# Running sums of a depthwise convolution kept in a PSUM bank instead of SBUF

## The chip, the core and the metric

The kernel runs on one core of one Trainium2 chip. It is a single launch, and the metric is the time on the device in microseconds. The instructions go to five engines that run beside each other and wait for each other through semaphores: TensorE (PE in the rows, PEld for its weight loads), VectorE (DVE), ScalarE (ACT), GpSimd (POOL) and SyncE (SP), which issues transfers.

## The reference, cut to what matters

The program computes two layers of a hybrid block (convolution, retention and window attention side by side, 256 positions, 1024 channels), and behind them a second block with a recurrence, a Fourier mix and a mixture of experts. The change touches one operation of the first two layers, the depthwise convolution of 31 taps:

```python
def conv_module(u_glu, gate, dw, db, ln_g, ln_b):
    a, b = jnp.split(u_glu, 2, axis=-1)
    v = a * jax.nn.sigmoid(b)
    y = lax.conv_general_dilated(
        v, dw[:, None, :].astype(v.dtype), window_strides=(1,),
        padding=[(CONV_KERNEL // 2, CONV_KERNEL // 2)],
        dimension_numbers=('NWC', 'WIO', 'NWC'),
        feature_group_count=CONV_WIDTH) + db.astype(v.dtype)
...
    mu = jnp.mean(yf, axis=-1, keepdims=True)
    var = jnp.mean(jnp.square(yf - mu), axis=-1, keepdims=True)
    yf = (yf - mu) * lax.rsqrt(var + EPS) * ln_g.astype(jnp.float32) + ln_b.astype(jnp.float32)
    y = jax.nn.silu(yf).astype(v.dtype)
    return y * jax.nn.silu(gate)
```

## The kernel before

Channels lie on the 128 partitions and positions along the free dimension, so the 1024 channels are 8 column blocks `k` of 128 × 256. `vpad` holds v of all 8 with 15 zeros at either side, `dw` the taps as per-partition scalars. `conv_taps` takes a pair of column blocks (four pairs `q` in a layer) and adds up 31 shifted products on VectorE: tap 0 is a `tensor_scalar` (product plus bias), taps 1 to 30 are `scalar_tensor_tensor`, out = vpad shifted × scalar + running sum. The running sum `acc[k]` is an SBUF tile; its buffers are called C1_0 to C1_7, and C in the trace. The two column blocks of a pair take turns, so a tap needs the result of the instruction two places ahead of it.

The program is one long list in the order in which a planner (`Sched`) emits it. The main generator (`layer`) emits TensorE's work, weight block by weight block. Beside it run tasks (`spawn`), each a generator that yields between pieces: with priority 0 they bring results out of PSUM, with 1 they are attention and retention chains, and the convolution's tasks have priority 2, the lowest. `pump` steps tasks whose condition holds and whose planned time has come, `force` steps one where the main list waits. The planner holds a cost for each instruction and a finishing time for each engine; what an engine then executes is strictly in the emitted order. Costs depend on where operands lie, and the low halves of the split weights (`wlo` = `wraw` − `whi`) go to VectorE or GpSimd as its times say.

Of the eight PSUM banks four (`pbulk`, tiles pb) take the large products and four (`pside`, tiles ps) serve attention, retention and statistics. `conv_taps` uses none before. Its results are awaited twice: `conv_fin` starts with eight products of `acc` by `ones` on TensorE (a mean over channels), and in the merge the attention output (products of A by `whi` and `wlo`) waits for `pairs + taps`, since its tile takes the place of `vpad`. The gate products (H by `whi` and `wlo`) stand ahead of it. The retention branch (`hd0`, `hd1`) normalises its rows on VectorE with groups of a BN_STATS, a BN_AGGR, a dozen instructions one column wide (`rs_ub`, `rs_yb`) and one that applies it.

Each record of an engine's work goes through one helper, line 192, so the rows are told apart by their tiles.

Of the kernel before, what the change touches and what calls it, by code (L numbers as in the profile page):

```python
# [328 lines left out]
class Kern:  # L329
# [370 lines left out]
        self.tbs.put(sg)  # L700
        self.pbulk.put(pa, pb)

    def conv_taps(self, l, q, glu):
        V, par = self.dve, self.par[l]
        vpad, acc = self.vpad, self.acc
        yield lambda: glu.done
        dwc = lambda j, k: self.dw[l][(j * 8 + k) // 124][:, (j * 8 + k) % 124:(j * 8 + k) % 124 + 1]
        for j in range(31):
            for k in (2 * q, 2 * q + 1):
                if j == 0:  # L710
                    V.tensor_scalar(
                        out=acc[k], in0=vpad[:, k, 0:256], scalar1=dwc(0, k), scalar2=par[:, 32 + k:33 + k],
                        op0=ALU.mult, op1=ALU.add)
                else:
                    V.scalar_tensor_tensor(
                        out=acc[k], in0=vpad[:, k, j:j + 256], scalar=dwc(j, k), in1=acc[k],
                        op0=ALU.mult, op1=ALU.add)
            if j % 2 == 0:
                yield

    def h_tiles(self):
# [334 lines left out]
    def layer(self, l):  # L1056
        s, A, par = self.s, self.A, self.par[l]
# [27 lines left out]
        for c in range(2):  # L1085
            def done(i, pb):
                agt.append(self.evac(self.silu_task(ag[c * 4 + i * 2:c * 4 + i * 2 + 2], pb)))
            yield from self.form_b(h, 8, done)
# [12 lines left out]
        taps, cgt = [], []  # L1101
        for q in range(4):
            got = {}
            def done(i, pb):
                got[i] = pb
                if i == 1:
                    taps.append(s.spawn(self.conv_taps(l, q, self.evac(self.glu_task(q, got[0], got[1]))), 2))
            yield from self.form_b(h, 8, done)
        cg = self.parts("C2")
        for q in range(2):  # L1110
            def done(i, pb):
                cgt.append(self.evac(self.silu_task(cg[4 * q + 2 * i:4 * q + 2 * i + 2], pb)))
            yield from self.form_b(h, 8, done)
# [1952 lines left out]
```

## Time and profile before

| | us |
|---|---|
| median of 3 runs | 2966.68 (2962.86 to 2969.67) |
| the profiled execution's own time | 2963.53 |
| its span | 2961.8 |

| engine | busy us | share of the span | instructions |
|---|---|---|---|
| PE | 2531.1 | 85% | 16380 |
| DVE | 1737.0 | 59% | 3380 |
| POOL | 789.1 | 27% | 544 |
| ACT | 757.3 | 26% | 1307 |

The shares are means over stages with different limits. The two layers take the first 1600 us or so, the experts most of the rest. A stretch is read by which engine is hardly ever idle in it. In the trace's orders of time a row joins equal instructions that follow each other: its first number is the start, its second the time from the first one's start to the last one's end, and x the count. A last bracket names idle time of the engine ahead of it and what ended it.

### The profile page before, as it was taken

Reading aid. Unit: us, or ns where it says so; the run is one execution under the profiler, and the core shown is the slowest. Engines: PE = TensorE matmul, PEld = TensorE weight load, DVE = VectorE, ACT = ScalarE, POOL = GpSimd, SP = SyncE. Lnnn points to the kernel's source line nnn. Section 1 sums busy time; section 2 is a strip of 40 time slices with the busy share of each in tenths; the row PEclk is TensorE's granted clock in tenths of the full one; section 3 lists DMA queues with packets and bytes.
Section 4 is the critical chain, followed back from the end, with each engine's and each line's share of the span. In section 5 each row is a group of like instructions: output and inputs, shape, how many; then the busy total and the mean of one; then the engine's idle time right before and its main releaser. Section 6 shows DMA issues by size and latency. Waiting matters only on the chain. (4 is left out here: it accounts for less than half of the span.)

```text
span 2961.8 us, 43624 instructions
## 1 busy us (share of the span) xinstructions
PE 2531.1 (85%) x16380; PEld 1649.1 (56%) x16380; DVE 1737.0 (59%) x3380; ACT 757.3 (26%) x1307; POOL 789.1 (27%) x544
## 2 busy tenths in 40 slices
PE   6887777679998876788989986699999999999784
PEld 3767656568978765578978564443433323333111
DVE  3769999977458899986466747522332323323213
ACT  2432332244444432334433211110100100001000
POOL 3325444545235454544322214200000000000000
PEclk9888888899999988899988987699999999999987
DMA  7354333334654333335562352489999999999996
GB/s 253 89 206 149 108 93 93 100 106 150 202 170 128 99 107 100 100 114 159 182 237 94 103 145 98 139 323 362 408 409 409 408 406 407 404 405 406 404 407 252
DMA packets 267314, 661.43 MB, mean 223 GB/s; under 512 B 48098, under 2 KB 66030, under 8 KB 265944
## 3 DMA queue, kind: packets, MB, share of 16 engines
q1 hardware_dynamic: 255616, 633.46, 60.0%
q0 software_dynamic: 6240, 22.05, 2.0%
q10 hardware_dynamic: 5240, 3.06, 0.4%
q8 instruction: 131, 2.15, 0.3%
q14 instruction: 87, 0.71, 0.1%
HBM read 640.63 MB, written 17.86 MB: 222 GB/s over the span
## 5 line engine op out<-in xcount | busy, mean ns | idle before, releaser
L192 POOL TENSOR_TENSOR wlo<-wraw,whi 128x1024 fp32r<-128x1024 f32 (+1 forms) x211 | 520.3, 2482 | 653.9 <-ACT whi L192 586.6
L192 PE MATMUL pb<-H,whi 128*128 128x256 f32 x2784 | 551.3, 300 | 31.1 <-ACT whi L192 10.3
L192 PEld LDWEIGHTS pb<-H,whi 128*128 128x128 f32 x2784 | 466.1, 205 | 44.3 <-issue 23.4
L192 ACT CAST whi<-wraw 128x1024 fp32r<-128x1024 f32 (+1 forms) x352 | 359.9, 1041 | 457.0 <-PE pb L192 279.3
L192 PE MATMUL pb<-H,wlo 128*128 128x256 f32 x1392 | 412.2, 296 | 25.3 <-POOL wlo L192 18.7
L192 DVE SCALAR_TENSOR_TENSOR C<-vpad,dw,C 128x256 f32<-128x256 f32 x480 | 350.3, 797 | 0.0
L192 DVE TENSOR_TENSOR wlo<-wraw,whi 128x1024 fp32r<-128x1024 f32 (+1 forms) x141 | 193.1, 1376 | 201.4 <-ACT whi L192 191.1
L192 PEld LDWEIGHTS pb<-H,wlo 128*128 128x128 f32 x1392 | 284.7, 204 | 28.3 <-POOL wlo L192 21.3
L192 POOL TENSOR_TENSOR mf<-mf,mx 128x512 f32<-128x512 f32 x2 | 3.2, 1640 | 1026.7 <-DVE mf L192 1026.7
L192 PE MATMUL pb<-wraw,mx 128*32 128x256 f32 (+1 forms) x1680 | 254.3, 493 | 25.8 <-DMA wraw<-in_w 25.2
L192 PE MATMUL pb<-whi,H 128*128 128x512 f32 x704 | 245.7, 421 | 0.0
L192 PE MATMUL pb<-wraw,maT 128*64 128x512 f32 (+1 forms) x920 | 201.8, 612 | 8.2 <-DMA wraw<-in_w 7.6
L192 PEld LDWEIGHTS pb<-wraw,mx 128*32 128x32 f32 (+1 forms) x1680 | 75.2, 123 | 162.0 <-issue 81.1
L192 ACT ACTIVATE ms<-mg 128x256 f32<-128x256 f32 (+1 forms) x78 | 29.1, 373 | 526.3 <-DVE mg L192 509.8
L192 PEld LDWEIGHTS pb<-whi,H 128*128 128x128 f32 x704 | 141.1, 200 | 35.1 <-issue 3.0
L192 DVE TENSOR_SCALAR mg<-pb 128x256 f32<-128x256 f32 (+1 forms) x59 | 21.8, 369 | 224.8 <-PE pb L192 224.8
L192 PE MATMUL pb<-wlo,H 128*128 128x512 f32 x352 | 145.0, 412 | 7.8 <-POOL wlo L192 7.0
L192 DVE SCALAR_TENSOR_TENSOR my<-pb,msg,my 128x512 fp32r<-128x512 f32 x29 | 21.8, 751 | 170.1 <-ACT my L192 169.6
L192 PEld LDWEIGHTS pb<-wraw,maT 128*64 128x64 f32 (+1 forms) x920 | 47.7, 127 | 122.4 <-issue 63.9
L192 PE MATMUL ps<-cst_base,t 128*128 128x128 f32 x208 | 43.6, 338 | 78.3 <-DVE t L192 46.3
L192 DVE TENSOR_TENSOR mf<-ps,mf 128x512 f32<-128x512 f32 x117 | 76.3, 684 | 54.1 <-PE ps L192 48.7
L192 PE MATMUL ps<-wraw,mx 128*32 128x256 f32 (+1 forms) x568 | 91.9, 506 | 5.8 <-DMA wraw<-in_w 5.6
(652 smaller groups left out, 4302.2 us busy)
## 6 DMA issues: line engine op xcount, KB each, us to landing
wraw<-in_w SPq DMA_DIRECT2D x580, 512.0 KB, 10.1
wraw<-in_w_in SPq DMA_DIRECT2D x228, 512.0 KB, 4.0
whi<-in_w SPq DMA_DIRECT2D x95, 512.0 KB, 10.1
wlo<-in_w SPq DMA_DIRECT2D x93, 512.0 KB
wraw<-in_w_ada SPq DMA_DIRECT2D x48, 512.0 KB, 5.3
wraw<-in_w_in SPq DMA_DIRECT2D x68, 256.0 KB, 3.9
wraw<-in_w_ret_out SPq DMA_DIRECT2D x32, 512.0 KB, 4.0
wraw<-in_w_out SPq DMA_DIRECT2D x24, 512.0 KB, 5.9
```

Of the source, the lines that this page charges most:

```text
L192: r = f(*a, **k)
```

## The change

`conv_taps` takes one bank of `pside`. The running sums of its two column blocks are the two halves of that bank, from tap 0 to tap 29; tap 30 reads them there and writes `acc[k]` in SBUF. The bank is given back behind the last tap. A task starts only when the tasks of the earlier pairs are done (`before`) and a bank of `pside` is free, so that at most one bank is held. The arithmetic is the same, in the same order.

```diff
-    def conv_taps(self, l, q, glu):
+    def conv_taps(self, l, q, glu, before):
+
         V, par = self.dve, self.par[l]
         vpad, acc = self.vpad, self.acc
-        yield lambda: glu.done
+        yield lambda: glu.done and all(k.done for k in before) and len(self.pside.free) > 0
+        ps = self.pside.get()
+        z = {2 * q: ps[:, 0:256], 2 * q + 1: ps[:, 256:512]}
...
                     V.tensor_scalar(
-                        out=acc[k], in0=vpad[:, k, 0:256], scalar1=dwc(0, k), scalar2=par[:, 32 + k:33 + k],
+                        out=z[k], in0=vpad[:, k, 0:256], scalar1=dwc(0, k), scalar2=par[:, 32 + k:33 + k],
...
                     V.scalar_tensor_tensor(
-                        out=acc[k], in0=vpad[:, k, j:j + 256], scalar=dwc(j, k), in1=acc[k],
+                        out=acc[k] if j == 30 else z[k], in0=vpad[:, k, j:j + 256], scalar=dwc(j, k), in1=z[k],
...
             if j % 2 == 0:
+                if j == 30:
+                    self.pside.put(ps)
                 yield
...
-                    taps.append(s.spawn(self.conv_taps(l, q, self.evac(self.glu_task(q, got[0], got[1]))), 2))
+                    taps.append(s.spawn(self.conv_taps(l, q, self.evac(self.glu_task(q, got[0], got[1])), list(taps)), 2))
```

The order changes in the two layers only. VectorE, near the start of the taps in the first layer, with the waits that an instruction has; DVE_49 is VectorE's own semaphore. R are attention's rotated inputs, C the running sums. Before:

```order
L192 SCALAR_TENSOR_TENSOR C_0_1982<-vpad,dw_603,C_0_1982 128x256
L192 SCALAR_TENSOR_TENSOR C_1_1983<-vpad,dw_603,C_1_1983 128x256
L192 SCALAR_TENSOR_TENSOR C_0_1982<-vpad,dw_603,C_0_1982 128x256 [waits DVE_49]
L192 SCALAR_TENSOR_TENSOR C_1_1983<-vpad,dw_603,C_1_1983 128x256 [waits DVE_49]
L192 TENSOR_TENSOR R_0_1924<-R_0_1922,R_1_1923 128x192
```

The same place now:

```order
L192 SCALAR_TENSOR_TENSOR ps_2232<-vpad,dw_603,ps_2232 128x256
L192 SCALAR_TENSOR_TENSOR ps_2232<-vpad,dw_603,ps_2232 128x256 [waits DVE_49] x3
L192 COPY A_0_1647<-ps_2433 128x256 [waits PE_49]
L192 COPY A_1_1648<-ps_2433 128x256
L192 TENSOR_TENSOR R_0_1924<-R_0_1922,R_1_1923 128x192
```

Every tap but the first of a group waits for the tap just ahead of it, also where that one wrote the other half of the bank; before, the third and fourth waited for the first and second.

VectorE at the end of the first layer's taps, before (t are retention's rows, ps products of retention):

```order
L192 SCALAR_TENSOR_TENSOR t_5_5012<-ps_5014,bmv,R_0_4521 128x512
L192 SCALAR_TENSOR_TENSOR C_6_1988<-vpad,dw_605,C_6_1988 128x256
L192 SCALAR_TENSOR_TENSOR C_7_1989<-vpad,dw_605,C_7_1989 128x256
L192 SCALAR_TENSOR_TENSOR C_6_1988<-vpad,dw_605,C_6_1988 128x256
L192 SCALAR_TENSOR_TENSOR C_7_1989<-vpad,dw_605,C_7_1989 128x256
L192 BN_STATS bst<-ps_5139 128x6
```

Now (left out between the rows with "...", two normalisation groups):

```order
L192 SCALAR_TENSOR_TENSOR t_6_4928<-ps_5023,bmv,R_0_4503 128x512
L192 SCALAR_TENSOR_TENSOR ps_4942<-vpad,dw_603,ps_4942 128x256 x8
L192 TENSOR_TENSOR R_0_5146<-ps_5147,R_0_5145 128x512
L192 SCALAR_TENSOR_TENSOR ps_4942<-vpad,dw_603,ps_4942 128x256 x4
L192 TENSOR_TENSOR R_0_5146<-ps_5168,R_0_5145 128x512
L192 SCALAR_TENSOR_TENSOR ps_4942<-vpad,dw_603,ps_4942 128x256 x4
...
L192 SCALAR_TENSOR_TENSOR ps_4942<-vpad,dw_603,ps_4942 128x256 x8
L192 SCALAR_TENSOR_TENSOR t_4_5179<-ps_5185,t_4_5179 128x512
L192 SCALAR_TENSOR_TENSOR ps_4942<-vpad,dw_605,ps_4942 128x256 x12
...
L192 SCALAR_TENSOR_TENSOR ps_4942<-vpad,dw_605,ps_4942 128x256 x12
...
L192 SCALAR_TENSOR_TENSOR ps_4942<-vpad,dw_605,ps_4942 128x256 x6
L192 SCALAR_TENSOR_TENSOR C_6_1988<-vpad,dw_605,ps_4942 128x256
```

With the last one, for C_7, 56 taps of the fourth pair now stand behind the group that ends in t_6; before, the taps of the four pairs were interleaved, and four were left behind the group that ends in t_5.

TensorE at the same place, before (gate products, then `ones`, then more gate products; the attention output follows 24 rows later):

```order
L192 MATMUL pb_5023<-H_817,wlo 128x256
L192 MATMUL ps_5139<-R_0_4519,t_3_4931 128x512 x2
L192 MATMUL ps_5144<-C_0_1982,ones 128x256
...
L192 MATMUL ps_5144<-C_7_1989,ones 128x256
L192 MATMUL pb_5022<-H_817,whi 128x256
```

Now:

```order
L192 MATMUL pb_4992<-H_817,wlo 128x256
L192 MATMUL ps_5147<-cst_base,t_5_4927 128x128
...
L192 MATMUL ps_5185<-R_4159 128x256 x4
L192 MATMUL ps_5205<-R_1_4502,t_4_5179 128x512 x2
L192 MATMUL ps_5241<-R_1_4502,t_4_5179 128x512 x2
...
L192 MATMUL ps_5292<-C_0_1982,ones 128x256
...
L192 MATMUL ps_5292<-C_7_1989,ones 128x256
...
L192 MATMUL pb_5307<-A_0_3425,whi 128x256
```

The gate products all stand ahead of the `ones` now, and between them come only retention's last products; the attention output stands right behind.

## Rows read from the trace of the kernel before

**Rows 1.** Busy time by stretch; columns are named in the first line.

```profile
core 0: us, PE busy (x) PEld busy (x) DVE busy (x) ACT busy (x) POOL busy (x), PEclk, DMA share, GB/s
268.00:635.00 367.00, 267.60 (x1431) 219.57 (x1430) 345.13 (x623) 116.57 (x197) 168.72 (x80) 0.85 0.35 99
635.00:925.00 290.00, 268.69 (x1922) 251.49 (x1921) 184.07 (x278) 128.40 (x179) 126.24 (x70) 0.98 0.53 166
925.00:1290.00 365.00, 284.69 (x1620) 239.05 (x1619) 338.86 (x585) 131.03 (x213) 189.28 (x87) 0.88 0.36 104
```

**Rows 2.** Groups of VectorE instructions: busy us, mean ns, idle time before.

```profile
L192 DVE SCALAR_TENSOR_TENSOR C<-vpad,dw,C 128x256 f32<-128x256 f32 x480 | 350.3, 797 | 0.0
L192 DVE TENSOR_SCALAR C<-vpad,dw,par 128x256 f32<-128x256 f32 x16 | 11.3, 746 | 0.0
```

**Rows 3.** Instructions of tile C: shortest/median/longest ns, first and last start.

```profile
L192 DVE SCALAR_TENSOR_TENSOR C<-vpad,dw,C x480: 465/475/2633, 279.9 to 1287.8; 128x256 f32<-128x256 f32 x160
L192 DVE TENSOR_SCALAR C<-vpad,dw,par x16: 394/404/2483, 268.4 to 1055.5; 128x256 f32<-128x256 f32 x16
L192 DVE TENSOR_TENSOR C<-vpad,C x16: 418/422/427, 782.9 to 1468.7; 128x256 fp32r<-128x256 f32 x16
```

**Rows 4.** VectorE in order of time, runs of taps in the first layer.

```profile
557.90 13.21 DVE L192 SCALAR_TENSOR_TENSOR C<-vpad,dw,C 128x256 f32<-128x256 f32 x12
...
571.63 6.41 DVE L192 SCALAR_TENSOR_TENSOR C<-vpad,dw,C 128x256 f32<-128x256 f32 x16
...
581.75 16.57 DVE L192 SCALAR_TENSOR_TENSOR C<-vpad,dw,C 128x256 f32<-128x256 f32 x20
```

**Rows 5.** GpSimd in order of time, the same stretch.

```profile
559.67 9.97 POOL L192 TENSOR_TENSOR wlo<-wraw,whi 128x1024 fp32r<-128x1024 f32 x4 [4.67 <-ACT whi L192]
583.61 10.07 POOL L192 TENSOR_TENSOR wlo<-wraw,whi 128x1024 fp32r<-128x1024 f32 x4 [13.97 <-ACT whi L192]
```

**Rows 6.** Instructions that read PSUM tiles (ps, pb), columns as in rows 3.

```profile
L192 DVE SCALAR_TENSOR_TENSOR LK<-ps,par,LK x8: 473/480/486, 106.3 to 1561.7; 128x256 f32<-128x256 f32 x8
...
L192 DVE TENSOR_SCALAR tmp<-pb,gb x16: 536/542/545, 53.5 to 1508.3; 128x256 f32<-128x256 f32 x16
L192 DVE SCALAR_TENSOR_TENSOR H<-pb,par,H x16: 474/483/484, 98.7 to 849.4; 128x256 fp32r<-128x256 f32 x16
...
L192 DVE TENSOR_TENSOR C<-pb,tb x16: 401/410/425, 331.6 to 1032.7; 128x256 f32<-128x256 f32 x16
```

**Rows 7.** VectorE in order of time, in the experts.

```profile
2408.13 0.43 DVE L192 SCALAR_TENSOR_TENSOR mg<-ml,mg 128x256 f32<-128x256 f32 x1 [0.21 <-ACT ms L192]
2408.59 0.42 DVE L192 TENSOR_TENSOR ma<-mg,ms 128x256 f32<-128x256 f32 x1
2408.93 0.42 DVE L192 TENSOR_SCALAR mg<-pb 128x256 f32<-128x256 f32 x1
```

**Rows 8.** Instructions that write wlo, columns as in rows 3.

```profile
L192 POOL TENSOR_TENSOR wlo<-wraw,whi x211: 1253/2422/6308, 45.9 to 1581.5; 128x1024 fp32r<-128x1024 f32 x104, 128x512 fp32r<-128x512 f32 x2
L192 DVE TENSOR_TENSOR wlo<-wraw,whi x141: 692/1226/3427, 50.7 to 1853.7; 128x1024 fp32r<-128x1024 f32 x140, 128x512 fp32r<-128x512 f32 x1
```

**Rows 9.** VectorE in order of time, end of the first layer's taps.

```profile
629.59 0.68 DVE L192 BATCH_NORM_STATS2 bst<-ps 128x6 f32<-128x512 f32 x1
...
633.38 1.66 DVE L192 SCALAR_TENSOR_TENSOR C<-vpad,dw,C 128x256 f32<-128x256 f32 x4
```

**Rows 10.** TensorE in order of time: gates, ones and A; A in the second layer.

```profile
625.97 1.16 PE L192 MATMUL pb<-H,whi 128*128 128x256 f32 x2
...
637.07 3.62 PE L192 MATMUL ps<-C,ones 128*128 128x256 f32 x16
...
643.37 0.40 PE L192 MATMUL pb<-A,whi 128*128 128x256 f32 x2
...
1280.80 0.68 PE L192 MATMUL pb<-A,whi 128*128 128x256 f32 x1
```

**Rows 11.** TensorE's groups from 643 to 693 us, columns as in rows 2.

```profile
L192 PE MATMUL ps<-R,t 128*128 128x512 f32 x8 | 3.8, 593 | 0.0
L192 PE MATMUL ps<-cst_base,t 128*128 128x128 f32 x12 | 2.0, 277 | 2.8 <-ACT t L192 2.8
```

## Prediction

> **What bounds the kernel now.** I read the stretches first [rows 1]. From 268 to 635 us (first layer) and from 925 to 1290 us (second), VectorE is busy 345 of 367 us and 339 of 365 us, TensorE only 268 and 285 us: VectorE sets the pace there. In the 290 us behind the first of them it is the other way round: TensorE 269 us, VectorE 184. The changed work, the 31 taps of the depthwise convolution over 8 column blocks, lies entirely in the two stretches: 480 SCALAR_TENSOR_TENSOR and 16 TENSOR_SCALAR [rows 2], 240 and 8 in each layer.
>
> Then I looked at one tap. Its mean is 797 ns, its median 475 and its longest 2633 [rows 2, 3], for always the same shape. The order of time shows why: 16 taps in a row took 6.41 us while GpSimd was idle, 12 took 13.21 us while it ran four `wlo` subtractions of about 2.5 us, and 20 took 16.57 us under four more [rows 4, 5]. A tap that meets a running GpSimd operation waits for its end, some 2 us. The operations of VectorE with one input in PSUM show no such wait, though they run in the same stretches: their longest and shortest times differ by 10 to 24 ns [rows 6]. They include one of the tap's own form, with a per-partition scalar (473 to 486 ns).
>
> **The change part by part**, as time of VectorE, both layers together, against the profiled execution (2963.5 us, span 2961.8; the median of the runs, 2966.7, lies 3.2 us above it).
>
> 1. *The sums are in PSUM, so a tap has one SBUF input and no longer waits for GpSimd.* 480 × (797 − 475) ns = 154.6 us and 16 × (746 − 404) ns = 5.5 us [rows 2, 3]: **−160 us**. The tap itself keeps 475 ns: forms with a PSUM source of this width take 410 to 483 ns [rows 6], those without 422 to 475 [rows 3]. That VectorE writes PSUM is not in this trace; I bound the tap from below by 410 ns and from above by the slowest 256-wide row with a PSUM source, 542 ns [rows 6], which is −31 or +32 us, and take 475, the row that is the same operation. [...]
>
> 2. *Two blocks share one bank, and every tap now waits for the one just ahead of it.* The order shows the wait on nearly every row; before, a tap waited for the one two places ahead. The price is in the start-to-start times: without a wait on its neighbour the next instruction starts before the first has ended (taps: (6.41 − 0.47)/15 = 0.396 us for a tap of 0.475 [rows 3, 4]; the pair 2408.59 and 2408.93 us: 0.34 for 0.42), with it 0.03 to 0.04 us after its end (2408.13 and 2408.59: 0.46 for 0.43) [rows 7]. So a tap takes 0.475 + 0.035 = 0.51 instead of 0.396 us: 480 × 0.114 = **+55 us**. The first of each group has no such wait, which makes 40 the lower end.
>
> 3. *GpSimd still runs.* An operation of 2.42 us [rows 8] that no longer holds up a tap can hold up the next VectorE instruction with two SBUF inputs. Where taps stand in runs of 8 or 12 it ends inside the run; a group of 4 takes 2.0 us and doesn't cover it. I give back a quarter of the 160, **+40 us**; none and half (80) are the ends.
>
> 4. *What the new order puts into the stretch.* The blocks run one after the other, so the last tap of a layer now stands behind three more normalisation groups of the retention branch (3.8 us each, from 629.59 to the next tap at 633.38 [rows 9]) and some 4 us of its other steps: 15 us a layer, +31. The planner also turns 15 `wlo` subtractions in the two stretches over to VectorE: 15 × (1.226 − 0.083) = +17 us [rows 8], and 12 fewer stand on GpSimd there. Four of them held up a run of taps by 13.21 − 12 × 0.40 = 8.4 us, 2.1 each [rows 4, 5]; I take 1.5 for any of them, −18. Together **+30 us**.
>
> 5. *Idle time of VectorE.* Now 22 and 26 us [rows 1]. Its work falls by 160 − 55 − 40 − 30 = 35 us, which brings it near TensorE's in the middle of the stretch; there VectorE will wait for TensorE at times. I take 30 us a layer: **+12**; from −10 to +40.
>
> 6. *The end of the stretch.* Here something new is late. The sums over `acc` (`ones`) need the last tap, and TensorE works in order, so the attention output (`A`) waits behind them. Before, TensorE went from the first gate product at 625.97 through the `ones` at 637.07 to the first `A` product at 643.37, without a pause [rows 10]. Now 56 taps of the last block, two normalisation groups and 4 us of scaling follow the last gate product's neighbours on VectorE: 56 × 0.51 + 7.6 + 4 = 40 us, with TensorE nearly idle: `A` starts some 38 us later behind the gates than before. VectorE's time for this is in the terms above already; it only lies in one place. What comes on top: in the first layer 8.3 us stood between the end of the last tap (633.38 + 1.66 [rows 9]) and `A`, for gate products, and in the new order only the `ones` and four transposes, some 4.6 (−4). In the second layer `A` started at 1280.8, ahead of the last tap's start at 1287.8 [rows 3, 10], and will start 4.6 us behind its end (+14): **+10 us**.
>
> 7. *Behind it.* The retention steps that moved ahead are gone from the stretch that TensorE bounds: in the first 50 us of it they held TensorE 2.0 + 3.8 us and stood in most of its pauses [rows 11], and a few microseconds return: −6 us a layer, **−12 us**.
>
> Sum: −160 + 55 + 40 + 30 + 12 + 10 − 12 = **−25 us**; 2963.5 − 25 = 2938.5, and on the scale of the medians **2942 us**. From about 1600 us on both programs have the same order; nothing changes there.
>
> **The rivals.**
>
> *The turn at the bank costs more than the speed brings (slower).* The mechanism is term 6: early blocks that are done faster don't help if TensorE can't use the time before the last block. The sum of −25 is made of +76 at the ends of the two layers (38 each), −12 behind them and so −89 ahead of them. If TensorE, busy 73 and 78% of the stretches [rows 1], or the attention chains, which have one bank fewer, let only 60% of the 89 through, 36 us are missing: 2978. It decides as soon as more than 25 of the 89 are lost. For it: that share of TensorE. Against it: the granted clock is only 0.85 and 0.88 there [rows 1], so TensorE's work has some room to shrink.
>
> *The waits move to other instructions (no change).* Term 3 at 40% instead of 25% is +24 us: 2966. For it: other VectorE work is about half of the stretch. Against it: many of its instructions read PSUM and can't be held up [rows 6].
>
> *The semaphore between neighbours costs nothing (faster).* Then term 2 is gone: 2942 − 55 = 2887. The rows speak against it [rows 7]. [...]
>
> *A tap into PSUM is slow (slower).* At 542 ns, the upper bound of term 1, the time is 2942 + 32 = 2974.
>
> *The change doesn't do what it says.* If a tap with one SBUF input still waits for GpSimd, since its scalar also lies in SBUF, the 160 stays and the quarter of term 3 falls away: 2942 + 160 − 40 = 3062. The forms with such a scalar and no spread [rows 6] speak against it.
>
> **How the numbers follow.** Chances: forecast, 2915 to 2957, 0.52; turn at the bank 0.20; waits move 0.14; no cost of the semaphore 0.05; slow tap 0.05; no effect 0.04. A change of 0.2% (6 us) is about what a measurement of this kernel can tell from none. Faster: 0.48 of the forecast and the 0.05, 0.53. Same: 0.04 of the forecast, 0.05 of the bank's turn, 0.11 of the moved waits, 0.02 of the slow tap, 0.22. Slower: the rest of these, 0.15 + 0.03 + 0.03, and 0.04, 0.25. The range for 8 in 10 reaches from the forecast with less given back by GpSimd's operations (2942 − 37 = 2905) to the bank's turn with some of the slower tap (2982). The forecast's own range, 2915 to 2957, stands beside it.
>
> **What would show it.** In the profile after: the median and the mean of a tap near each other (475 to 485 ns; a longest of over 1 us refutes term 1); runs of taps at 0.51 us from start to start (0.40 refutes term 2); other VectorE instructions with two SBUF inputs waiting longer in sum than now, by some 40 us; a pause of TensorE of 30 to 45 us ahead of the `ones` products of both layers, with VectorE busy; the first `A` product some 10 to 20 us earlier than 643 us. If `A` comes later than 643 us, term 3 or 5 was too small, and the bank's turn has decided.

## The result and the profile after

The changed kernel takes 2910.57 us (median of 4 runs, 2907.73 to 2912.84); the kernel before, run beside it, 2964.77. The ratio is 0.9824 (0.9809 to 0.9838): 48 to 57 us faster, where the prediction had 25.

The stretches of the profiled execution (2911.1 us; columns as in [rows 1]): first to last tap of the first layer, from there to the first tap of the second, its taps, and from its last tap to 1554.7 us, where the last product of H by `whi` of the program starts, some 100 us into the second block (1606.3 us before). That product is the marker for the end of the layers below. A marker belongs to one execution: ahead of the first tap VectorE's order is the same in all programs here, and the first tap still starts at 262 to 270 us, so a few microseconds between two markers mean nothing.

```profile
265.00:624.20 359.20, 272.04 (x1469) 221.01 (x1468) 307.26 (x680) 125.57 (x211) 155.54 (x77) 0.86 0.36 105
624.20:899.80 275.60, 258.55 (x1858) 244.66 (x1858) 170.75 (x231) 119.53 (x163) 109.18 (x63) 0.97 0.53 169
899.80:1248.80 349.00, 279.79 (x1594) 231.71 (x1593) 303.73 (x647) 136.54 (x221) 152.92 (x76) 0.90 0.37 109
1248.80:1554.70 305.90, 292.12 (x2503) 273.44 (x2502) 186.59 (x261) 128.20 (x194) 102.59 (x78) 0.94 0.53 175
```

Against [rows 1], the stretches of the taps are only 8 and 16 us shorter, though VectorE (the DVE column) is busy 38 and 35 us less. The two stretches behind them, in which no tap runs, have become 14 and 10 us shorter. Before, the last one read:

```profile
1290.40:1606.30 315.90, 294.04 (x2477) 273.45 (x2476) 198.52 (x309) 133.35 (x202) 107.27 (x80) 0.94 0.51 170
```

From there to the end of the program both take the same (1355.5 and 1356.4 us). So the gain was made in the two layers, and half of it lies where the prediction looked for almost none.

The taps after, instruction groups (busy us, mean ns) and then the same with shortest/median/longest ns:

```profile
L192 DVE SCALAR_TENSOR_TENSOR ps<-vpad,dw,ps 128x256 f32<-128x256 f32 x464 | 226.5, 488 | 13.4
L192 DVE TENSOR_SCALAR ps<-vpad,dw,par 128x256 f32<-128x256 f32 x16 | 8.7, 544 | 0.3
L192 DVE SCALAR_TENSOR_TENSOR C<-vpad,dw,ps 128x256 f32<-128x256 f32 x16 | 7.0, 478 | 0.3
```

```profile
L192 DVE SCALAR_TENSOR_TENSOR ps<-vpad,dw,ps x464: 468/490/491, 274.4 to 1247.3; 128x256 f32<-128x256 f32 x155
...
L192 DVE TENSOR_SCALAR ps<-vpad,dw,par x16: 533/545/549, 265.1 to 1200.1; 128x256 f32<-128x256 f32 x16
```

The 2633 ns of [rows 3] are gone: no SCALAR_TENSOR_TENSOR of the taps is longer than 491 ns. Tap 0, a TENSOR_SCALAR, isn't held up any more either (longest 549 ns, 2483 in [rows 3]), but into PSUM it takes 545 ns instead of 404. GpSimd still runs 156 and 153 us beside the taps. The price shows in the order of time (start, time to the last one's end):

```profile
584.23 4.15 DVE L192 SCALAR_TENSOR_TENSOR ps<-vpad,dw,ps 128x256 f32<-128x256 f32 x8
...
610.20 6.25 DVE L192 SCALAR_TENSOR_TENSOR ps<-vpad,dw,ps 128x256 f32<-128x256 f32 x12
```

(6.25 − 0.49)/11 = 0.524 us from start to start, against 0.396 before [rows 4].

TensorE at the end of the first layer's taps; the bracket names its pause and what ended it:

```profile
600.38 6.41 PE L192 MATMUL ps<-R,t 128*128 128x512 f32 x8 [10.87 <-DVE t L192]
611.10 0.48 PE L192 MATMUL ps<-cst_base,t 128*128 128x128 f32 x1 [4.30 <-ACT t L192]
621.05 0.90 PE L192 MATMUL ps<-cst_base,t 128*128 128x128 f32 x3 [9.48 <-ACT t L192]
621.75 5.90 PE L192 MATMUL ps<-C,ones 128*128 128x256 f32 x16
...
627.84 0.48 PE L192 MATMUL pb<-A,whi 128*128 128x256 f32 x2
```

The pauses ahead of `ones` add up to some 25 us here and 24 in the second layer, where the prediction had 30 to 45. `A` starts 15.5 us earlier than the 643.37 of [rows 10]; 10 to 20 were forecast.

**How VectorE's time is divided below.** Each instruction counts from its start to the next one's start; what lies more than 0.04 us behind its end is idle. "Held up" is the time of an instruction above the lower quartile of its own form; it doesn't tell by what. Over both tap stretches:

| us, both layers | before | new order, SBUF sums | after | two banks |
|---|---|---|---|---|
| taps | 356 | 345 | 249 | 197 |
| of that held up | 163 | 151 | 0 | 1 |
| other instructions | 340 | 372 | 392 | 414 |
| of that held up | 85 | 67 | 85 | 107 |
| idle | 35 | 54 | 66 | 72 |
| last product of H by `whi` at | 1606.3 | 1619.1 | 1554.7 | 1525.1 |

The second and the fourth column are experiments, which follow.

### The profile page after: what moved, and what is told of

Its sections match the earlier page's. It is cut to its first block, busy times and chain, and to the rows that moved or that the text cites. A ratio compares the mean times of both kernels' runs of the same rounds, so it can differ in the third digit from the quotient of the medians.

```text
span 2911.1 us, 43619 instructions
## 1 busy us (share of the span) xinstructions
PE 2521.5 (87%) x16380; PEld 1638.1 (56%) x16380; DVE 1641.5 (56%) x3402; ACT 758.5 (26%) x1307; POOL 720.3 (25%) x522
## 5 line engine op out<-in xcount | busy, mean ns | idle before, releaser
L192 POOL TENSOR_TENSOR wlo<-wraw,whi 128x1024 fp32r<-128x1024 f32 (+1 forms) x189 | 456.8, 2429 | 608.9 <-ACT whi L192 566.4
L192 PE MATMUL pb<-H,whi 128*128 128x256 f32 x2784 | 537.9, 295 | 18.0 <-DVE vpad L192 10.8
L192 PEld LDWEIGHTS pb<-H,whi 128*128 128x128 f32 x2784 | 454.6, 200 | 29.4 <-issue 23.6
L192 PE MATMUL pb<-H,wlo 128*128 128x256 f32 x1392 | 405.3, 291 | 16.2 <-POOL wlo L192 12.5
L192 DVE TENSOR_TENSOR wlo<-wraw,whi 128x1024 fp32r<-128x1024 f32 (+1 forms) x163 | 234.3, 1441 | 222.9 <-ACT whi L192 216.1
L192 PEld LDWEIGHTS pb<-H,wlo 128*128 128x128 f32 x1392 | 277.6, 199 | 18.6 <-POOL wlo L192 14.4
L192 DVE SCALAR_TENSOR_TENSOR ps<-vpad,dw,ps 128x256 f32<-128x256 f32 x464 | 226.5, 488 | 13.4
```

Source lines behind the costliest of these rows:

```text
L192: r = f(*a, **k)
```

## The experiments

**The new order alone.** The sums go back to SBUF and everything else stays: the instructions stand in the same order on all engines as in the changed kernel (the planner is given the cost that tap 0 has with a PSUM output).

```diff
-        z = {2 * q: ps[:, 0:256], 2 * q + 1: ps[:, 256:512]}
+        z = {k: acc[k] for k in (2 * q, 2 * q + 1)}
```

> The changed kernel with its order kept instruction for instruction on all engines, but the running sums in SBUF again (the bank is taken and left unused). It separates the new order from the new place of the sums. Theory A (what the two profiles show: taps took 356 us from start to start before and 249 us after, other VectorE instructions of the same stretches were held up 85 us before and 85 us after): the sums' place is worth about 107 us of VectorE's time and nothing is handed on to other instructions, while the order costs; then this kernel shows taps of 750 ns and more on the mean, other instructions still held up by 70 to 90 us, and a time of 2990 to 3020 us, above the kernel before. Rival B (the forecast's own bill: place -65 us, order +40): 2975 to 3010 us, but with the other instructions held up by only 45 to 60 us. Rival C (the order is neutral and only moves work): 2960 to 2970 us, as before.

Measured: 2972.74 us, 1.0022 of before (1.0011 to 1.0033), 3 to 10 us slower. The taps are held up again:

```profile
L192 DVE SCALAR_TENSOR_TENSOR C<-vpad,dw,C 128x256 f32<-128x256 f32 x480 | 339.9, 774 | 0.0
```

The other instructions are held up 67 us, between B's range and A's. The time lies between rival C's and theory A's, below B's: the order costs something, but little. So the new place of the sums, at the same order, is worth 0.9824/1.0022 = 0.9802, 59 us of time, or 64 us at the last product of H: 96 off the taps, of which 21 went to other instructions (18 as held-up time) and 12 to idle time. Theory A's "nothing is handed on" falls with that, since the table's 85 and 85 were at two orders. What the order does by itself is seen in this kernel's stretches:

```profile
265.00:656.50 391.50, 274.43 (x1489) 222.80 (x1489) 356.84 (x680) 126.17 (x211) 164.49 (x78) 0.85 0.34 97
656.50:932.30 275.80, 259.32 (x1861) 245.58 (x1860) 170.05 (x232) 119.93 (x164) 108.86 (x63) 0.96 0.53 168
932.30:1311.80 379.50, 288.61 (x1590) 236.35 (x1589) 343.66 (x646) 136.14 (x221) 160.12 (x75) 0.87 0.34 100
1311.80:1619.00 307.20, 291.38 (x2504) 273.86 (x2503) 186.80 (x261) 128.52 (x195) 102.18 (x78) 0.94 0.53 174
```

The tap stretches are 25 and 14 us longer than before, the two behind them 14 and 9 us shorter. In the stretch from 656 us TensorE has 259 us of work instead of 269 and 16 us of pauses instead of 21; in the last one 291 instead of 294, and 16 instead of 22.

**Two banks for a block.** Each column block of a pair has its own bank, so that a tap waits for the one two places ahead.

```diff
-        yield lambda: glu.done and all(k.done for k in before) and len(self.pside.free) > 0
-        ps = self.pside.get()
-        z = {2 * q: ps[:, 0:256], 2 * q + 1: ps[:, 256:512]}
+        yield lambda: glu.done and all(k.done for k in before) and len(self.pside.free) > 1
+        ps = [self.pside.get(), self.pside.get()]
+        z = {2 * q + i: ps[i][:, 0:256] for i in range(2)}
```

> The changed kernel with one PSUM bank for each of the two column blocks of a pair, so a tap waits for the one two places ahead, as before. Term 2 of the forecast: the pitch of taps falls from 0.525 to about 0.40 us, 60 us less of VectorE's time in both layers. Theory A: VectorE is still what the stretches wait for (33 us idle in each), half of it reaches the end: 2870 to 2890 us. Rival 1 (the wait for the neighbour costs nothing): the pitch stays at 0.52 and the time at 2910 us. Rival 2 (the attention chains, left with two banks, run later): pitch 0.40, but 2910 us or more, with longer pauses of TensorE ahead of products into ps.

Measured: 2894.95 us, 0.9763 of before (0.9738 to 0.9787). Twelve taps in a row now take

```profile
594.14 4.79 DVE L192 SCALAR_TENSOR_TENSOR ps<-vpad,dw,ps 128x256 f32<-128x256 f32 x12
```

(4.79 − 0.48)/11 = 0.392 us each, and the taps 52 us less. The last product of H comes 29.6 us earlier than in the changed kernel, theory A's half; the rest goes to other instructions that are held up now (22 us) and to idle time. The time itself is only 16 us shorter, outside A's range: in the profiled execution 13 of the 29.6 us were lost behind the layers, where the order is the same (last section).

**A program of taps alone.** Sections of 48 taps, with GpSimd idle or with eight subtractions of 128x1024 beside them.

> A small program of its own that computes nothing of the reference: sections of 48 taps of 128x256 in two alternating sums, each once with GpSimd idle or with eight GpSimd subtractions of 128x1024 beside it. Sums in SBUF: 0.40 us a tap (19 us) with GpSimd idle; with GpSimd, each of the eight operations holds up one tap for about 2 us: 33 to 37 us. Sums in the two halves of one bank: 0.525 us a tap (25 us), the same with and without GpSimd. In two banks: 0.40 (19 us), the same with and without. One sum in SBUF, one in a bank: by theory A eight waits again (33 to 36 us), by its rival four (26 us). Input from SBUF, output to PSUM: held up if two SBUF inputs decide (33 us or more), free if the place of the output decides (19 us). Input from PSUM, output to SBUF: free (19 to 20 us).

The groups over the whole program (busy us, mean ns; sumA and sumB with GpSimd idle and running, one and two likewise, the others with GpSimd running):

```profile
L31 DVE SCALAR_TENSOR_TENSOR one<-src,sc,one 128x256 f32<-128x256 f32 x96 | 47.0, 490 | 3.3
L31 DVE SCALAR_TENSOR_TENSOR sumB<-src,sc,sumB 128x256 f32<-128x256 f32 x48 | 31.2, 649 | 0.0
...
L31 DVE SCALAR_TENSOR_TENSOR mixA<-src,sc,mixA 128x256 f32<-128x256 f32 x24 | 25.1, 1045 | 0.0
L31 DVE SCALAR_TENSOR_TENSOR twoB<-src,sc,twoB 128x256 f32<-128x256 f32 x48 | 23.2, 484 | 0.0
...
L31 DVE SCALAR_TENSOR_TENSOR wrB<-src,sc,sumB 128x256 f32<-128x256 f32 x24 | 19.9, 827 | 0.0
...
L31 DVE SCALAR_TENSOR_TENSOR mixB<-src,sc,mixB 128x256 f32<-128x256 f32 x24 | 11.5, 479 | 0.0
L31 DVE SCALAR_TENSOR_TENSOR rdB<-src,sc,inB 128x256 f32<-128x256 f32 x24 | 11.2, 468 | 0.0
```

Start of the SBUF section with GpSimd, in order of time, and the one-bank section without and with it:

```profile
21.29 2.43 DVE L31 SCALAR_TENSOR_TENSOR sumA<-src,sc,sumA 128x256 f32<-128x256 f32 x1
23.64 2.56 DVE L31 SCALAR_TENSOR_TENSOR sumB<-src,sc,sumB 128x256 f32<-128x256 f32 x1
...
57.73 25.16 DVE L31 SCALAR_TENSOR_TENSOR one<-src,sc,one 128x256 f32<-128x256 f32 x48
...
83.30 25.16 DVE L31 SCALAR_TENSOR_TENSOR one<-src,sc,one 128x256 f32<-128x256 f32 x48
```

| 48 taps, us in all | GpSimd idle | running | longer than 1 us |
|---|---|---|---|
| sums in SBUF | 18.96 | 35.62 | 8 |
| halves of one bank | 25.16 | 25.16 | 0 |
| two banks | 18.77 | 18.89 | 0 |
| one in SBUF, one in a bank | | 32.67 | 8 |
| both inputs SBUF, output PSUM | | 35.66 | 8 |
| one input PSUM, output SBUF | | 18.88 | 0 |

All six came out as expected, the fourth by theory A but slightly below its range (33). For this form it is the inputs that decide, not where the result goes (35.66 us with both in SBUF and the output in PSUM, 18.88 with one in PSUM and the output in SBUF); beside the sums in SBUF each of the eight GpSimd operations, 19.70 us in all, held up one tap to its end (2.43 to 2.56 us); and the wait for the neighbour costs 0.525 − 0.392 = 0.13 us. No run puts two tiles into one bank, so whether the bank or the shared tile makes the wait isn't shown.

**Half of the sums in PSUM**, again in the changed kernel's order on all engines (with the same help for the planner).

```diff
-        z = {2 * q: ps[:, 0:256], 2 * q + 1: ps[:, 256:512]}
+        z = {2 * q: ps[:, 0:256], 2 * q + 1: acc[2 * q + 1]}
```

> The changed kernel, same order on all engines, with the first column block of each pair summed in the PSUM bank and the second in SBUF: neighbours don't depend on each other, and half of the taps can be held up. Theory A (a GpSimd operation holds up the next instruction with two SBUF inputs, whichever comes): every second tap is such an instruction, so nearly every GpSimd operation still finds one; the SBUF taps have a mean of 1.0 us or more, the PSUM taps stay below 0.5 us, pitch of free taps about 0.40 us, and the time lies within 25 us of the kernel with all sums in SBUF. Rival (each tap is held up by its own chance): the loss halves, the time lies in the middle between that kernel and the changed one or below, as the waits between neighbours (55 us) are gone too.

Measured: 2950.95 us, 0.9956 (0.9942 to 0.9969), 20 us below the kernel with SBUF sums and 40 above the changed one.

```profile
L192 DVE SCALAR_TENSOR_TENSOR C<-vpad,dw,C 128x256 f32<-128x256 f32 x240 | 223.0, 929 | 0.0
L192 DVE SCALAR_TENSOR_TENSOR ps<-vpad,dw,ps 128x256 f32<-128x256 f32 x232 | 111.3, 480 | 0.1
```

Half as many taps are still held up 116 us instead of 151, 77%, although no tap waits for its neighbour. The mean of 929 ns is below the 1.0 us expected, the rest is theory A's: a half measure doesn't take half of the loss away, since the next tap that can be caught is caught.

**Without the turn, and at a higher priority.** The first starts a block as soon as a bank is free, with several banks held; the second lifts the convolution's tasks to the priority of attention and retention, so that the last block ends earlier.

```diff
-        yield lambda: glu.done and all(k.done for k in before) and len(self.pside.free) > 0
+        yield lambda: glu.done and len(self.pside.free) > 0
```

> The changed kernel without the turn: a block starts as soon as any bank of the four is free, and several blocks hold a bank each. Sums stay in PSUM; the subtractions for wlo are given out nearly as in the kernel before (208 to GpSimd, 144 to VectorE). Theory A (the turn's order costs about 9 us, as the run with SBUF sums in the new order showed): without it 2895 to 2905 us. Rival (attention and retention lack the banks that the blocks hold): 2915 us or more, with TensorE's and VectorE's pauses ahead of ps longer than in the changed kernel.

```diff
-                    taps.append(s.spawn(self.conv_taps(l, q, self.evac(self.glu_task(q, got[0], got[1])), list(taps)), 2))
+                    taps.append(s.spawn(self.conv_taps(l, q, self.evac(self.glu_task(q, got[0], got[1])), list(taps)), 1))
```

> The changed kernel with the convolution's tasks at the priority of the attention and retention chains, so that the last block ends before TensorE has run out of gate products (in the order the products by ones stand behind the first of A instead of ahead of them in the first layer). Theory A (VectorE is what the stretches wait for, so it doesn't matter where in them its taps lie; the pause of TensorE ahead of ones only shows where the wait falls): 2903 to 2918 us. Rival (that pause, some 30 us a layer, is the price of the turn): 2870 to 2895 us. A third case (the chains that now step back are late instead): above 2918 us.

Measured: 2910.30 us (0.9829, 0.9809 to 0.9849) without the turn, 2912.53 (0.9844, 0.9825 to 0.9862) with the priority. The first lies between theory and rival. Its tap stretches are 317 and 324 us, 43 and 25 shorter than the changed kernel's, and the ones behind them 51 and 13 us longer: the last product of H comes at 1554.6 us, the changed kernel's at 1554.7. The second is what theory A expected: TensorE's pauses between the last gate product and `ones` fell from 27 and 29 us to 0 and 5, and the median stayed. (Its profiled execution, the fastest of its four, reached the last product of H at 1545.7 us, 9 earlier than the changed kernel's.) With one bank a block, where in a layer the taps lie and where the pause falls shows little in the time. Neither run shows its change alone, though: the planner also leaves 19 and 12 more subtractions to GpSimd than in the changed kernel (208 and 201 against 189), and in the last experiment 19 more go with 12 us less.

**Two banks and the priority.**

> The same priority with two banks a block, the fastest so far (2895 us). Theory A: within 8 us of it, 2887 to 2903. Rival (the pause ahead of ones is a loss): 2860 to 2880 us. Third case (attention, with two banks and a lower place, is late): above 2903 us.

Measured: 2868.67 us, 0.9699 (0.9666 to 0.9732), the fastest of all, about 40 us ahead of the changed kernel; below theory A's range, in the rival's. In the layers the priority gained 16.6 us over the kernel with two banks (last product of H at 1508.5); the other 12 of the 29 us between the two profiled executions are the time that was lost behind the layers there. The pauses between the last gate product and `ones` are 8 and 5 us here against 22 and 22 with two banks alone, 31 less in all. So here the rival may hold in part, that the pause is a loss; the run doesn't part it from 14 more subtractions on GpSimd (204 against 190). Its tap stretches:

```profile
265.00:599.00 334.00, 259.98 (x1428) 213.07 (x1426) 285.59 (x643) 120.56 (x204) 162.02 (x79) 0.88 0.39 112
880.00:1190.00 310.00, 265.20 (x1570) 222.66 (x1569) 271.40 (x602) 132.04 (x215) 171.81 (x83) 0.93 0.42 123
```

**What VectorE's time is worth.** The taps 1 to 29 are left out.

```diff
-        for j in range(31):
+        for j in (0, 30):
```

> The changed kernel without taps 1 to 29 of every column block: 464 of the 480 are left out, 464 x 0.525 = 244 us of VectorE's time. It shows how far time taken off VectorE reaches the end at all. TensorE is busy 272 and 280 us of the stretches of 359 and 349. Theory A (VectorE's time passes in full until TensorE's own work is all that is left): a gain of 110 to 150 us, 2760 to 2800. Rival (the stretches hang on chains of small steps on all engines): a gain below 80 us, above 2830.

One execution: 2812.1 us, 98 less than the changed kernel, between the two expectations. With the taps gone, TensorE is still busy only 265 of 315 us (from the first tap to the first product of `A`):

```profile
270.00:585.00 315.00, 264.86 (x1480) 215.04 (x1478) 231.41 (x462) 134.43 (x230) 151.59 (x85) 0.93 0.40 116
851.00:1154.00 303.00, 272.18 (x1589) 226.54 (x1588) 224.18 (x425) 137.13 (x232) 165.76 (x88) 0.95 0.40 121
```

So a microsecond taken off the taps is worth less and less at the last product of H: 64 of 96 (from SBUF to one bank), 30 of 52 (to two banks), 103 of 234 (from one bank to none); the last two steps change the order as well.

**`wlo` back to GpSimd.** The planner is told to favour GpSimd by 1 us in the layers, in the changed kernel and in the one with two banks and the priority.

```diff
-    L = (1.5, 1.0, 2.0, 3.2, 0.0)
-    L1 = (1.5, 1.0, 1.0, 2.9, 0.0)
+    L = (1.5, 1.0, 2.0, 3.2, 1.0)
+    L1 = (1.5, 1.0, 1.0, 2.9, 1.0)
```

> The changed kernel with the planner's bias for GpSimd raised by 1 us in both layers: 208 of the wlo subtractions on GpSimd and 144 on VectorE, nearly as in the kernel before (211 and 141), instead of 189 and 163; the order of TensorE stays within 274 of 13641 rows. It tests the forecast's term 4. VectorE saves 19 x (1.226 - 0.083) = 22 us. Theory A (with the sums in PSUM a GpSimd operation holds up VectorE by only 85 us / 151 operations = 0.56 us): 11 us come back, net -11 on VectorE, 2897 to 2906 us. The forecast's price (1.5 us for each GpSimd operation): 19 x 1.5 = 28, net +6: 2913 to 2920 us. A third case (VectorE's work moves without effect): 2907 to 2913.

> Two banks a block, the convolution at the chains' priority, and the same bias: 219 wlo subtractions on GpSimd and 133 on VectorE (204 and 148 without the bias, 2869 us). Theory A: 15 x (1.143 - 0.6) = 8 us less of VectorE's time, 2855 to 2869 us. The forecast's price of 1.5 us: 2869 to 2880 us.

Measured: 2898.57 us (0.9779, 0.9755 to 0.9803) for the first, as theory A had it. Other instructions were held up 84 us, as in the changed kernel (85), although 19 more operations ran on GpSimd: one costs VectorE no more than about half a microsecond now (85 us over 151 operations), not 1.5. The second took 2879.17 (0.9736, 0.9698 to 0.9775), 10 us more than without the bias, but its interval overlaps that kernel's (0.9666 to 0.9732), so a loss isn't clear. The price that the rival names doesn't show: other instructions were held up 97 us, against 99 without the bias. VectorE's idle time in the second layer rose from 31 to 43 us, in another order; this wasn't followed up.

## Why the prediction was half right

The direction and the mechanism were right, and the time lies in the wide range (2905 to 2982); the size was not, 25 us instead of 52 at the last product of H (54 by the medians), and the time is below the forecast's own range of 2915 to 2957. By its steps, with the place of the sums and the order taken apart by the first experiment:

| us | predicted | measured |
|---|---|---|
| 1, 2: taps, contention gone, chained waits | −160 + 55 = −105 | −96 |
| 3: handed on to other instructions | +40 | +21 (held up: +18) |
| 5: idle time of VectorE | +12 | +12 |
| **place of the sums** | **−53** | **−63** |
| 4: order, VectorE's work in the tap stretches | +30 | +20 (other instructions +32, taps −11) |
| idle time of VectorE that the order brought | none | +19 |
| 6, 7: order, outside the tap stretches | −4 + 14 − 12 = −2 | −26 |
| **order** | **+28** | **+13** |

The measured numbers are those of the traces, one execution each; at the last product of H they come to −64 and +13, −52 together. The steps that failed are terms 6 and 7, 24 us too high, and term 3, 19 too high; the idle time, 19 more than term 5 allows, made up for part of it.

*Terms 1 and 2* held: no SCALAR_TENSOR_TENSOR over 491 ns where "over 1 us" would have refuted them, and 0.525 us from start to start for the 0.51 forecast. A tap into PSUM takes 490 ns with the wait and 484 without it, against 475 [rows 3]. Only tap 0 was slower than the sum had it (545 ns for 404, 2 us in all). From start to start a source and an output in PSUM cost a tap nothing: 48 taps take 18.77 us in two banks against 18.96 in SBUF. The wait for the neighbour does cost: 25.16 us with it against 18.77 without it for the same 48. The rival that it costs nothing is out.

*Term 3* was mis-sized: a quarter of the 160 was given back, and 18 us were held up elsewhere. My reading, argued and not shown by a run of its own, is that a GpSimd operation holds up only what comes while it runs and can be held, and that most of the time that it used to take off a tap now passes under taps that can't. The prediction's "two SBUF inputs" is too narrow for what can be held: tap 0 has one and took up to 2483 ns [rows 3]. Term 4 priced GpSimd's operations at 1.5 us for the same reason and took 18 us off for the twelve that moved to VectorE; with taps out of reach they hold up no more than half a microsecond each, and moving them costs: 12 us come back when 19 go back to GpSimd.

*Term 5* fits its row by the way the rows are cut. It had +12 for the idle time of the whole change; the idle time rose by 31 (35 to 66), 19 of it with the order.

*Terms 6 and 7* are where most of the miss lies. Behind the first layer's taps they had −4 − 6 = −10 us, and −14 came; behind the second layer's they had 14 − 6 = +8, and −9 came. (The other 3 us lie ahead of the first tap, where VectorE's order is the same.) Term 6 took the start of `A` as the end of the stretch and charged 14 us in the second layer, because `A` started ahead of the last tap before and starts behind it now. It does, 3.7 us behind its end, but TensorE works in order (there the `ones` start at 1246.23 us and `A` at 1252.40) and was busy either way; what counts is its work behind the last tap. In the new order 48 of the 192 products of A by `whi` and `wlo` and some of the 16 by `ones` have moved behind it, 4.6 and 2.4 us of TensorE's time (from start to start), not 14; and retention's products (R by t, into R and t's transposes) have moved ahead, 6.2 us, so that these nearly cancel. TensorE's busy time there became 291 us instead of 294, the rest of that by the same products taking a little less time. The start of a group was the wrong marker; the work left behind the tap was the right one. Term 7 returned 6 us a layer for the moved retention steps, and the steps' own time was 7.4 and 6.2 us; but their pauses went with them, 5 and 6 us (21 to 16 and 22 to 16), which it left unpriced. In the last stretch before, they read

```profile
PE pb L192 <- ACT t L192: 5.0, 1, 5.0
...
PE ps L192 <- ACT t L192: 3.5, 1, 3.5
```

(who waited for whom, us in total, times, longest), and after there is no such row.

*The rival of the turn at the bank* did not come true: the time is below the forecast, not above it, and with the last block earlier the median is the same within 2 us. The pause ahead of `ones` is real, some 25 us a layer, and was forecast; with one bank a block taking it away brought nothing in the median, so it looks like the place where a wait falls. With two banks 31 us less of it went with 16.6 us less time, so the rival's mechanism isn't refuted altogether.

What stays open: what the turn costs by itself; why the higher priority brings 16.6 us in the layers with two banks and nothing in the median with one; and whether the bias that gains 12 us with one bank loses any with two.

## What to carry to other kernels

Price a change that also reorders in two sums, one at the new order with the old operands and one for the operands, and run the first: here the operands brought 59 to 64 us and the order cost 3 to 13, and somewhat more of the miss was in the second. Follow moved work to where it comes from: what the crowded stretch gets, another one loses, and a marker such as "the first product of A" says nothing unless the work on both sides of it is the same. And give each of two alternating sums its own bank, since a wait for the neighbour is paid on every instruction (0.13 us here).

## What the runs showed of the chip

A SCALAR_TENSOR_TENSOR of 128x256 with one input in PSUM isn't held up by GpSimd, also when its output lies in SBUF (48 in 18.88 us); with both inputs in SBUF it is, also when its output lies in PSUM (35.66 us). A TENSOR_SCALAR of that size, with its one tensor input in SBUF, was held up to 2483 ns when its output lay in SBUF [rows 3]; with its output in PSUM it wasn't (549 ns at most), but took 545 ns instead of 404.

TensorE's granted clock differed for the same work. The same 20 us of the second block, in the changed kernel and in the one with two banks, with TensorE busy in the 20 us ahead in both:

```profile
1590.00:1610.00 20.00, 19.26 (x144) 13.33 (x140) 16.62 (x54) 5.18 (x18) 4.93 (x13) 1.00 0.27 68
1610.00:1630.00 20.00, 19.11 (x160) 15.81 (x160) 15.25 (x53) 6.58 (x28) 4.93 (x11) 1.00 0.07 12
```

```profile
1560.00:1580.00 20.00, 19.46 (x147) 13.70 (x146) 16.25 (x52) 4.80 (x16) 5.31 (x13) 1.00 0.28 75
1580.00:1600.00 20.00, 19.07 (x96) 15.61 (x95) 10.54 (x36) 4.66 (x19) 2.26 (x5) 0.58 0.01 2
```

At 0.58 instead of 1.00, 96 products were done instead of 160, and 11 us were lost by 1620 us. The profiled execution without the turn shows the same at 1608 us (0.62), that of the fastest kernel doesn't (1.00 at 1562 us). No run here tells what sets it off; it is a reason to read the end of the layers, and not the time alone, when differences of 10 us are in question.
